# Start addresses of matmul operands in a transformer layer: three fillings in the pools

## The chip, the cores and the metric

The kernel runs on 1 core of a Trainium2 chip. The metric is the device time of one execution in microseconds (us). The kernel before takes 2929.12 us (median of 3 runs, 2928.11 to 2932.33).

## What is computed

One layer of a hybrid backbone over 1024 latent tokens of width 1024 with 256 context tokens, in float32. Cut to what matters here:

```python
p = h @ w_in                                    # h: modulated RMSNorm of x
att = neighbourhood_attention(q, k, v, k_ctx, v_ctx, rpb)
merged = (g0 * (att @ w_att_o) + g1 * (fourier @ w_fourier) + g2 * pooled)
x = x + gate1 * (merged @ w_out)
h2 = modulate(x, norm2_g, sh2, sc2)
affinity = softmax(h2 @ w_router)
gates, idx = lax.top_k(swapaxes(affinity, 1, 2), cap)   # 16 experts, 128 tokens each
xg = h2[idx]
a, u = xg @ w_gate[e], xg @ w_up[e]             # 1024 -> 2816
y = (silu(a) * u) @ w_down[e] * gates           # 2816 -> 1024
x = x + gate2 * scatter_add(y);  out = rmsnorm(x)
```

## The kernel before, in words

Every large product is made three times (lines 67 to 69, `mm3`): a float32 operand is split into a high part in the reduced type float32r and a remainder, and high x high, high x low, low x high are added up in PSUM. In a product one operand is stationary (128x128, loaded into the array) and one is moving (up to 512 columns are streamed past it).

A block of weights of 1 MB comes by DMA from the sync engine's queue into a raw buffer `wraw`; ScalarE casts it (line 62) and VectorE subtracts (line 63) into one of four buffers `whl` (high and low). The stages, in order of time:
- Projections, Fourier mixing, pooling, gates: the normed tokens `hT` (and `hcT` for the context) lie in SBUF in both parts. Most products have `hT` moving and `whl` stationary; for the values `whl` is moving and `hT` stationary.
- Attention, by head pairs.
- Merge (function `merge`): the attention's output is read back into tiles `at0` to `at7`, two pools of them (`attT0`, `attT1`, by halves of the tokens), as moving operand against `w_att_o` in `whl`. In the first chunk the first tile is read from a raw buffer of the ring instead. The sums, gated, go to `mg`; blocks of 128 tokens of it are split into `mhl`, the stationary operand of the product with `w_out` in `whl`. Then come norm, router and ranking; the ranking of groups of token blocks on VectorE runs beside the products of the next blocks.
- Experts (function `moe`): 16 experts one after the other. An expert's 128 rows are gathered (`xg`), transposed, modulated and split into `xT` (`turned`, 16 activations on ScalarE per expert but the first). The inner width 2816 goes in chunks of 512, the last of 256. Gate and up have `xT` stationary and `whl` moving; their gated product `a` is transposed on TensorE and split into `aT`, which is stationary for the down product with `whl` moving, into `y`. The result is scaled and added to the stream in memory by a scatter (line 1216, GpSimd), one per expert but the last. The loads run through a ring of 12 raw buffers, the splits 4 halves ahead. The order of TensorE, ScalarE and VectorE in this stage is written out by hand: the instructions stand in the order in which the loop calls for them.

Tiles lie in pools, each a run of bytes in every partition of SBUF. A tile's address follows from the pool's start and the tiles before it in the pool; pools on the right side grow from the top down. The names in the profile are the tiles' names without buffer numbers.

Of the kernel before, what the change touches and what calls it, by code (L numbers as in the profile page):

```python
# [9 lines left out]
F32 = mybir.dt.float32  # L10
# [24 lines left out]
def f(ap):  # L35
    return ap.bitcast(F32)


class Kernel:
# [13 lines left out]
    def pool(self, name, bufs=1, space=None, side=None):  # L53
        kw = {"reuse_waits": "tile"} if space != DRAM else {}
        if space is not None:
            kw["space"] = space
        if side is not None:
            kw["side"] = side
        return self.tc.tile_pool(name=name, bufs=bufs, **kw)

    def split(self, hi, lo, src, eng=None):
        self.nc.scalar.copy(hi, src)  # L62
        (eng or self.nc.vector).tensor_sub(lo, src, f(hi))  # L63
# [34 lines left out]
    def rstd(self, ss, pool, tag):  # L98

        nc = self.nc  # L100
        n = ss.shape[1]
        v = pool.tile([128, n], F32, name=tag + "v")
        s = pool.tile([128, n], F32, name=tag + "s")
        r = pool.tile([128, n], F32, name=tag + "r")
        nc.vector.tensor_scalar(v, ss, 1.0 / D, EPS, op0=ALU.mult, op1=ALU.add)
        nc.scalar.sqrt(s, v)
        nc.vector.reciprocal(r, s)
        nc.vector.tensor_mul(s, r, r)
        nc.vector.tensor_mul(s, s, v)
        nc.vector.tensor_scalar(s, s, -0.5, 1.5, op0=ALU.mult, op1=ALU.add)  # L110
        nc.vector.tensor_mul(r, r, s)
        return r
# [639 lines left out]
    def merge(self):  # L752
# [3 lines left out]
        self.tv = gates.tile([128, CB, NE, 4], F32R, name="tv")  # L756
        self.iota1 = gates.tile([128, 128], F32, name="iota1")
        with ExitStack() as st:
            rt = self.route_tiles(st.enter_context(self.pool("route")))
            mp = st.enter_context(self.pool("merged", side="right"))  # L760
            mg = [mp.tile([128, KT, 512], F32, name=f"mg{h}") for h in range(2)]
            xv = io["x"].rearrange("(r cb c) d -> cb r c d", r=R, cb=CB)
# [2 lines left out]
            def load(cb):  # L765
                mhl = hp.tile([128, 2, KT, 128], F32R, name="mhl")
                q = 128 * (cb % 4)
                self.split(mhl[:, 0], mhl[:, 1], mg[cb // 4][:, :, q:q + 128])
                tiles[cb] = mhl

            with ExitStack() as sa:
                ms = sa.enter_context(self.pool("msb", 2, side="right"))
                ap1 = sa.enter_context(self.pool("attT1", 1, side="right"))
                sa0 = sa.enter_context(ExitStack())
                ap0 = sa0.enter_context(self.pool("attT0", 1, side="right"))
                ps = sa.enter_context(self.pool("psa", 8, space=PSUM))
                for ch in range(2):
                    W = self.wchunk(io["w_att_o"], 512 * ch)
                    if ch == 0:
                        at0 = self.wraw.tile([128, 2048], F32R, name="wraw").rearrange("p (s t) -> p s t", s=2)  # L780
                        nc.sync.dma_start(f(at0), self.attd[0:128])
                        at = [[ap.tile([128, 2, 512], F32R, name=f"at{k}") for k in range(KT)]
                              for ap in (ap0, ap1)]
                        for k in [*range(1, KT), 0]:
                            for half in range(2):
                                nc.sync.dma_start(f(at[half][k]), self.attd[128 * k:128 * k + 128, :,
                                                                            512 * half:512 * half + 512])
                    units = [(b, half) for half in range(2) for b in range(4)]
                    acc = [ps.tile([128, 512], F32, name="mm") for _ in units]
                    order = [(k, u) for k in range(KT) for u in range(8)]  # L790
                    if ch:
                        order.sort(key=lambda ku: ku[1])
                    for k, u in order:
                        b, half = units[u]
                        p = acc[u]
                        i = 4 * ch + b
                        ws, ts = slice(128 * b, 128 * b + 128), slice(512 * half, 512 * half + 512)
                        a = at0[:, :, ts] if ch == k == 0 else at[half][k]
                        self.mm3(p, W(0, k)[:, ws], W(1, k)[:, ws], a[:, 0], a[:, 1], k == 0, k == KT - 1)
                        if k < KT - 1:  # L800
                            continue
                        sl = slice(128 * i, 128 * i + 128)
                        sg = ms.tile([128, 512], F32, name="sg")
                        pt = ms.tile([128, 512], F32, name="pt")
                        nc.sync.dma_start(sg, self.g1s[sl, ts])
                        nc.sync.dma_start(pt, self.part2[sl, ts])
                        nc.vector.tensor_mul(sg, p, sg)
                        nc.vector.tensor_add(mg[half][:, i], sg, pt)
                        if ch == 1 and u == 3:
                            sa0.close()  # L810
                            hp = st.enter_context(self.pool("mhl", 2))
                            w_out.append(self.wchunk(io["w_out"], 0))
                            load(0)
                            load(1)
            sp = st.enter_context(self.pool("x1", 2))
# [247 lines left out]
    def moe(self, upto):  # L1063
        nc, io = self.nc, self.io
        NR = RING
        with ExitStack() as st:
# [5 lines left out]
            sp = st.enter_context(self.pool("moe", 2))  # L1072
# [42 lines left out]
            def turned(ex, b, eng=None):  # L1115

                if b == 0:
                    ex.xT = sp.tile([128, 2, KT, 128], F32R, name="xT")
                scale, shift = self.mod2[:, 24:32], self.mod2[:, 0:8]
                tp = pst.tile([128, 512], F32, name="tp")  # L1120
                h32 = sp.tile([128, 512], F32, name="a")
                for k in range(4):
                    kk, cs = 4 * b + k, slice(128 * k, 128 * k + 128)
                    nc.tensor.transpose(tp[:, cs], ex.xg[:, 128 * kk:128 * kk + 128], self.ident)
                for k in range(4):
                    kk, cs = 4 * b + k, slice(128 * k, 128 * k + 128)
                    A, B = scale[:, kk:kk + 1], shift[:, kk:kk + 1]
                    nc.scalar.activation(ex.xT[:, 0, kk], tp[:, cs], AF.Identity, bias=B, scale=A)  # L1128
                    if eng is not None:
                        eng.tensor_scalar(h32[:, cs], tp[:, cs], A, B, op0=ALU.mult, op1=ALU.add)  # L1130
                    else:
                        nc.scalar.activation(h32[:, cs], tp[:, cs], AF.Identity, bias=B, scale=A)  # L1132
                nc.vector.tensor_sub(ex.xT[:, 1, 4 * b:4 * b + 4], h32.rearrange("p (k t) -> p k t", t=128),  # L1133
                                     f(ex.xT[:, 0, 4 * b:4 * b + 4]))
# [85 lines left out]
            def expert(e):  # L1220
                ex = Expert()
                ex.h, ex.aT = {}, {}
                ex.hot = choose_hot(e)
                return ex
# [8 lines left out]
            with self.pool("first", 1, side="right") as fp:  # L1233

                ex = expert(0)
# [6 lines left out]
            for b in range(2):  # L1242
                turned(ex, b, nc.vector)
# [7 lines left out]
            for j, (w, e, c, s) in enumerate(halves):  # L1251
                n = chunks[c][1]
                if (w, c, s) == ("w_gate", 0, 0) and e:
                    ex = nxt
# [23 lines left out]
                if (w, s) == ("w_gate", 0) and e + 1 < NE:  # L1278
                    if c == 2:
                        nxt = expert(e + 1)  # L1280
                        put(before, j + 3, lambda nx=nxt: choose_rows(nx))
                    if c == 4:
                        put(before, j + 1, lambda nx=nxt: turned(nx, 0))
                        put(before, j + 3, lambda nx=nxt: turned(nx, 1))
# [140 lines left out]
```

## Time and profile before

| | us |
|---|---|
| median of 3 runs | 2929.12 |
| lowest, highest | 2928.11, 2932.33 |
| profiled execution | 2928.25 |
| its span | 2926.5 |
| TensorE busy | 2811.0 |
| VectorE busy | 2040.7 |
| ScalarE busy | 1686.5 |
| GpSimd busy | 280.2 |

The span is the time from the first to the last instruction of the profiled execution. The stage of the experts takes the larger half of it, from 1334 us on. Matmuls are pipelined: a row of the timeline has the start of an instruction and how long it was in the engine, and the next one starts before it ends. So the engine's pace is read from the distance between starts. PE is TensorE, DVE VectorE, ACT ScalarE, POOL GpSimd, SPq the sync engine's DMA queue.

### The profile page before, as it was taken

The page shows a single profiled execution, that of the slowest core. Times are in us where ns is not written, and L with a number is a line of the kernel's source. Part 1 is how long each engine was busy: PE and PEld are TensorE (multiplying, and loading weights), DVE is VectorE, ACT ScalarE, POOL GpSimd, SP SyncE. Part 2 cuts the span into 40 slices and gives each one's busy share as a digit, 9 for nine tenths or more (in the row PEclk, how much of TensorE's full clock was granted, in tenths as well). Part 3 has the DMA queues.
Part 4 walks back from the last instruction along what each step waited for, and adds up shares of the span by engine and source line. Part 5 has one row for each costly group of instructions (what it writes and reads, how often), then busy time and mean ns, then how long its engine had stood idle before and what let it go on. Part 6 is the DMA issues. An engine that isn't in the chain of part 4 may idle for free.

```text
span 2926.5 us, 36071 instructions
## 1 busy us (share of the span) xinstructions
PE 2811.0 (96%) x13607; PEld 2304.4 (79%) x13607; DVE 2040.7 (70%) x2412; ACT 1686.5 (58%) x2005; POOL 280.2 (10%) x436
## 2 busy tenths in 40 slices
PE   7999999999999789987999999999999999999996
PEld 3888888887788777766888888888888888888885
DVE  4423232245578773478888988888888888988887
ACT  5412122212078771245777777777777777777775
POOL 1110000001144320000000000000000000000000
PEclk9999999999999899998999999999999999999998
DMA  8433231225877748558999999999999999999994
GB/s 250 175 124 144 79 123 66 104 80 167 272 190 193 184 140 284 156 166 309 338 362 369 375 367 360 370 376 365 358 367 382 365 361 360 385 364 360 362 383 175
DMA packets 346351, 783.54 MB, mean 268 GB/s; under 512 B 17288, under 2 KB 61008, under 8 KB 346048
## 3 DMA queue, kind: packets, MB, share of 16 engines
q1 hardware_dynamic: 326272, 713.48, 69.3%
q0 software_dynamic: 19664, 67.60, 6.9%
q8 instruction: 107, 1.75, 0.2%
q14 instruction: 68, 0.56, 0.1%
q10 hardware_dynamic: 240, 0.16, 0.0%
HBM read 710.37 MB, written 70.80 MB: 267 GB/s over the span
## 4 chain that ended last, share of the span: by engine, by line
PE 46%; ACT 4%; DVE 2%; issue 1%; DMA 1%; DVEq 0%
PE y L69 5%; PE y L68 5%; PE y L67 5%; PE w_gate L69 5%; PE w_gate L68 5%; PE w_gate L67 5%; PE w_up L67 5%; PE w_up L69 5%; PE w_up L68 5%; ACT whl L62 2%; PE tp L1202 1%; ACT a L1132 1%; ACT xT L1128 1%; DMA wraw<-in_w_up 1%; PE tp L1101 0%
## 5 line engine op out<-in xcount | busy, mean ns | idle before, releaser
L63 DVE TENSOR_TENSOR whl<-wraw,whl 128x2048 fp32r<-128x2048 f32 (+1 forms) x656 | 1295.1, 1997 | 240.4 <-ACT whl L62 236.3
L62 ACT CAST whl<-wraw 128x2048 fp32r<-128x2048 f32 (+1 forms) x660 | 1092.1, 1671 | 445.0 <-PE y L69 132.5
L68 PE MATMUL mm<-hT,whl 128*128 128x512 f32 x768 | 300.9, 392 | 1.6 <-DVE hT L273 1.6
L67 PE MATMUL mm<-hT,whl 128*128 128x512 f32 x768 | 300.2, 392 | 1.5 <-ACT hT L267 1.5
L69 PE MATMUL mm<-hT,whl 128*128 128x512 f32 x768 | 300.8, 392 | 0.0
L69 PE MATMUL w_gate<-whl,xT 128*128 128x512 f32 (+1 forms) x768 | 290.8, 379 | 2.8 <-DVE xT L1133 2.8
L67 PE MATMUL w_gate<-whl,xT 128*128 128x512 f32 (+1 forms) x768 | 292.1, 380 | 0.0
L67 PE MATMUL w_up<-whl,xT 128*128 128x512 f32 (+1 forms) x768 | 291.5, 380 | 0.0
L68 PE MATMUL w_gate<-whl,xT 128*128 128x512 f32 (+1 forms) x768 | 289.7, 377 | 0.0
L69 PE MATMUL w_up<-whl,xT 128*128 128x512 f32 (+1 forms) x768 | 289.1, 376 | 0.0
L68 PE MATMUL w_up<-whl,xT 128*128 128x512 f32 (+1 forms) x768 | 288.4, 375 | 0.0
L67 PE MATMUL y<-whl,aT 128*128 128x512 f32 x704 | 284.8, 405 | 0.0
L69 PE MATMUL y<-whl,aT 128*128 128x512 f32 x704 | 278.7, 396 | 0.0
L68 PE MATMUL y<-whl,aT 128*128 128x512 f32 x704 | 278.1, 395 | 0.0
L67 PEld LDWEIGHTS mm<-hT,whl 128*128 128x128 f32 x768 | 144.9, 189 | 37.8 <-ACT sg L529 5.2
L69 PEld LDWEIGHTS w_gate<-whl,xT 128*128 128x128 f32 x768 | 145.2, 189 | 32.2 <-DVE xT L1133 3.5
L68 PEld LDWEIGHTS mm<-hT,whl 128*128 128x128 f32 x768 | 145.3, 189 | 31.7 <-DVE hT L273 2.1
L69 PEld LDWEIGHTS mm<-hT,whl 128*128 128x128 f32 x768 | 145.2, 189 | 30.1
L68 PEld LDWEIGHTS w_gate<-whl,xT 128*128 128x128 f32 x768 | 145.0, 189 | 29.6
L69 PEld LDWEIGHTS w_up<-whl,xT 128*128 128x128 f32 x768 | 144.5, 188 | 29.1
L67 PEld LDWEIGHTS w_gate<-whl,xT 128*128 128x128 f32 x768 | 144.8, 189 | 28.4
L68 PEld LDWEIGHTS w_up<-whl,xT 128*128 128x128 f32 x768 | 144.3, 188 | 28.3
(354 smaller groups left out, 4333.1 us busy)
## 6 DMA issues: line engine op xcount, KB each, us to landing
wraw<-in_w_gate SPq DMA_DIRECT2D x160, 1024.0 KB, 11.1
wraw<-in_w_up SPq DMA_DIRECT2D x160, 1024.0 KB, 9.0
wraw<-in_w_down SPq DMA_DIRECT2D x160, 1024.0 KB, 11.8
wraw<-in_w_in SPq DMA_DIRECT2D x28, 1024.0 KB, 5.5
wraw<-in_ada_w SPq DMA_DIRECT2D x24, 1024.0 KB, 6.3
wraw<-in_w_gate SPq DMA_DIRECT2D x32, 512.0 KB, 11.4
wraw<-in_w_up SPq DMA_DIRECT2D x32, 512.0 KB, 8.5
wraw<-in_w_down SPq DMA_DIRECT2D x32, 512.0 KB, 4.9
```

The lines of the kernel that those rows point to most:

```text
L62: self.nc.scalar.copy(hi, src)
L63: (eng or self.nc.vector).tensor_sub(lo, src, f(hi))
L67: mm(out, lh, rh, start=start, stop=False, **kw)
L68: mm(out, lh, rl, start=False, stop=False, **kw)
L69: mm(out, ll, rh, start=False, stop=stop, **kw)
L1128: nc.scalar.activation(ex.xT[:, 0, kk], tp[:, cs], AF.Identity, bias=B, scale=A)
L1132: nc.scalar.activation(h32[:, cs], tp[:, cs], AF.Identity, bias=B, scale=A)
L1202: nc.tensor.transpose(tp[:, 128 * k:128 * k + 128], ex.ready[:, 128 * k:128 * k + 128], self.ident)
```

## The change

A method `fill` reserves a tile that nothing uses. It is called three times: 352 bytes at the end of the route tiles (ahead of all that is allocated after them in the merge, `mhl` among it), 416 bytes in the pool `msb` on the right side (below which the pools of `at` lie), and 352 bytes in the experts' pool, ahead of `xT`, once, with the first expert.

```diff
+    def fill(self, pool, size):
+        pool.tile([128, size // 4], F32, name="fill", bufs=1)
...
-            rt = self.route_tiles(st.enter_context(self.pool("route")))
+            rp = st.enter_context(self.pool("route"))
+            rt = self.route_tiles(rp)
+            self.fill(rp, 352)
...
                 ap1 = sa.enter_context(self.pool("attT1", 1, side="right"))
+                self.fill(ms, 416)
...
                 if b == 0:
+                    if ex.hot[0] == 0:
+                        self.fill(sp, 352)
                     ex.xT = sp.tile([128, 2, KT, 128], F32R, name="xT")
```

No instruction is added, removed or moved: on every engine and queue the built program has the same instructions in the same order with waits for the same semaphores. What differs is start addresses. The table has the byte at which an operand starts within a line of 512 bytes, as the built program has it; offsets within the tiles are whole lines in all of these.

| product (128 columns stationary) | products | moving, stationary | before | after |
|---|---|---|---|---|
| projections, 512 columns | 2304 | `hT`, `whl` | 64, 64 | 64, 64 |
| values, 512 columns | 480 | `whl`, `hT` or `hcT` | 64, 64 | 64, 64 |
| keys of the context, 256 columns | 192 | `hcT`, `whl` | 64, 64 | 64, 64 |
| pooling, 512 columns | 48 | `ph`, `wp` | 64, 320 | 64, 320 |
| attention output, first tile from the ring | 24 | `wraw`, `whl` | 480, 64 | 480, 64 |
| attention output | 360 | `at`, `whl` | 480, 64 | 64, 64 |
| merge with `w_out` | 384 | `whl`, `mhl` | 64, 224 | 64, 64 |
| experts' gate and up, 512 columns | 3840 | `whl`, `xT` | 64, 224 | 64, 64 |
| experts' gate and up, 256 columns | 768 | `whl`, `xT` | 64, 224 | 64, 64 |
| experts' down, 512 columns | 2112 | `whl`, `aT` | 64, 224 | 64, 64 |

Other tiles behind a filling move with it: `x1`, `xt`, `h2`, `g1b` of the merge and `a`, `yo` of the experts from 224 to 64, `x1T` (stationary in 64 router products of 16 columns) from 0 to 352.

## Rows read from the trace of the kernel before

**Rows 1.** Busy time: stretch, length, PE, PEld, DVE, ACT, POOL (instructions), clock, DMA share, GB/s.
```profile
1800.00:2300.00 500.00, 498.94 (x2366) 408.30 (x2365) 437.71 (x295) 380.01 (x340) 21.83 (x10) 1.00 1.01 367
```

**Rows 2.** Waits from 1400 to 2800 us: us in total, times, longest.
```profile
ACT whl L62 <- PE y L69: 120.3, 130, 2.1
...
SPq L1155 <- DVE whl L63: 934.2, 424, 5.3
```

**Rows 3.** Timeline of POOL: first and last scatter, 13 others between; start, us.
```profile
1460.82 3.41 POOL L1216 DMA_INDIRECT xacc<-yo,tok  x1 [76.96 <-DVE yo L1212]
...
2820.45 3.39 POOL L1216 DMA_INDIRECT xacc<-yo,tok  x1 [76.92 <-DVE yo L1212]
```

**Rows 4.** Timeline of PE, 340 to 380 us: first and last of 178.
```profile
339.83 0.39 PE L69 MATMUL mm<-hT,whl 128*128 128x512 f32 x1
...
379.95 0.39 PE L69 MATMUL mm<-hT,whl 128*128 128x512 f32 x1
```

**Rows 5.** Timeline of PE, 180 to 220 us: first and last of 178.
```profile
179.81 0.39 PE L68 MATMUL mm<-whl,hT 128*128 128x512 f32 x1
...
219.93 0.39 PE L68 MATMUL mm<-whl,hcT 128*128 128x512 f32 x1
```

**Rows 6.** Timeline of PE, 1110 to 1150 us: first and last of 173.
```profile
1109.66 0.40 PE L69 MATMUL mm<-at,whl 128*128 128x512 f32 x1
...
1149.96 0.39 PE L67 MATMUL mm<-at,whl 128*128 128x512 f32 x1
```

**Rows 7.** Timeline of PE, 1190 to 1208 us: first and last of 78.
```profile
1189.84 0.40 PE L68 MATMUL mm<-whl,mhl 128*128 128x512 f32 x1
...
1207.80 0.39 PE L67 MATMUL mm<-whl,mhl 128*128 128x512 f32 x1
```

**Rows 8.** Timeline of PE, 2865 to 2875 us, last expert: first and last of 44 products.
```profile
2864.70 0.39 PE L68 MATMUL w_gate<-whl,xT 128*128 128x512 f32 x1
...
2874.73 0.39 PE L69 MATMUL y<-whl,aT 128*128 128x512 f32 x1
```

**Rows 9.** Busy time in the stretches of rows 4 and 6 to 8; columns of rows 1.
```profile
340.00:380.00 40.00, 40.00 (x178) 33.10 (x178) 9.70 (x12) 8.09 (x11) 5.52 (x8) 1.00 0.41 146
...
1190.00:1208.00 18.00, 18.00 (x78) 14.48 (x78) 6.39 (x9) 1.70 (x2) 2.63 (x4) 1.00 0.47 171
1110.00:1120.00 10.00, 10.00 (x45) 8.03 (x44) 0.00 (x0) 0.00 (x0) 0.00 (x0) 1.00 1.05 387
2865.00:2875.00 10.00, 10.00 (x45) 7.99 (x44) 8.03 (x6) 5.37 (x5) 0.00 (x0) 1.00 0.00 0
```

**Rows 10.** Timelines of ACT and PE: the end of one expert.
```profile
2087.91 1.91 ACT L62 CAST whl<-wraw 128x2048 fp32r<-128x2048 f32 x1 [0.89 <-PE w_gate L69]
...
2099.55 0.40 PE L69 MATMUL y<-whl,aT 128*128 128x512 f32 x1
2100.13 0.63 PE L1202 MATMUL tp<-ident,a 128*128 128x128 f32 x4 [0.18 <-DVE a L1196]
```

**Rows 11.** Timeline of PE: 256 columns, 46 starts in the experts, 52 in the keys.
```profile
2103.76 0.28 PE L67 MATMUL w_gate<-whl,xT 128*128 128x256 f32 x1
...
2109.15 0.39 PE L67 MATMUL y<-whl,aT 128*128 128x512 f32 x1
...
162.84 0.28 PE L67 MATMUL mm<-hcT,whl 128*128 128x256 f32 x1
...
168.96 0.28 PE L67 MATMUL mm<-hcT,whl 128*128 128x256 f32 x1
```

**Rows 12.** Waits of DVE from 1240 to 1335 us.
```profile
DVE x L836 <- PE mm L69: 8.7, 6, 4.2
```

**Rows 13.** Busy time in 4 us inside an expert; columns of rows 1.
```profile
2030.00:2034.00 4.00, 4.00 (x19) 3.20 (x18) 3.90 (x3) 3.11 (x2) 0.00 (x0) 1.00 1.05 407
```

**Rows 14.** Timeline of PE: start of the products with `at`, 5 others between.
```profile
1101.41 0.79 PE L67 MATMUL mm<-at,whl 128*128 128x512 f32 x1 [2.97 <-DMA at<-attd]
...
1104.13 0.53 PE L67 MATMUL mm<-at,whl 128*128 128x512 f32 x1
```

## The prediction

> **What bounds the kernel now.** I read four views, in this order. The table of stretches says which engine is full: in the experts' stage TensorE (PE) is busy 498.94 of 500 us, VectorE (DVE) 437.71, ScalarE (ACT) 380.01, and the DMA engines carry 367 GB/s at a share of 1.01 [rows 1]. The waits say who is held by whom: ACT's casts of weights wait for PE to free a buffer (120.3 us behind `y` alone), and the load queue waits for DVE to free a slot of the ring (934.2 of 1400 us) [rows 2]. So loads and splits run ahead of PE, and PE's pace sets the time. The scatters, one per expert, give that pace: 14 periods between the first and the last shown, (2820.45 - 1460.82) / 14 = 97.1 us [rows 3]. The fourth view, PE's timeline, is the one that matters here. The change moves no instruction, only start addresses, so the question is whether a product's time depends on where its operands start. A row's duration does not tell, since products overlap; the distance from one start to the next does. I take it from the first and last start of an undisturbed stretch and the number of intervals between.
>
> **What a start address is worth.** All of these are products of 128x512, and the starts within a 512-byte line are those of the table in the section on the change.
> - Moving `hT` at 64, stationary `whl` at 64: 177 intervals, (379.95 - 339.83) / 177 = 226.7 ns [rows 4].
> - Moving `whl` at 64, stationary `hT` or `hcT` at 64, the roles as in the experts: (219.93 - 179.81) / 177 = 226.7 ns [rows 5].
> - Moving `at` at 480, stationary `whl` at 64: 172 intervals, (1149.96 - 1109.66) / 172 = 234.3 ns [rows 6].
> - Moving `whl` at 64, stationary `mhl` at 224: 77 intervals, (1207.80 - 1189.84) / 77 = 233.2 ns [rows 7].
> - Moving `whl` at 64, stationary `xT` or `aT` at 224: 43 intervals, (2874.73 - 2864.70) / 43 = 233.3 ns [rows 8].
>
> Equal starts give 226.7 ns in both roles, unequal ones 233 to 234. Other load does not explain it. The `at` stretch has 10 us in which DVE, ACT and GpSimd do nothing; the expert stretch has no DMA at all; and the `mhl` stretch (DVE 6.39 of 18 us, DMA 0.47) is loaded much like the `hT` stretch at 226.7 (DVE 9.70 of 40, DMA 0.41); the granted clock is 1.00 in all four [rows 9]. I therefore take 6.6 ns for an `xT`, `aT` or `mhl` product and 7.6 for an `at` product.
>
> A rule of the Trainium skill speaks against this. TensorE: Matmul & The Clock Gate, Part 2, on the steps of a matmul, says of the two read ports that "Loading the next tile's weights doesn't steal SBUF read bandwidth from the running matmul"; how the two addresses stand to each other would then not matter and the sum would be zero instead of what follows. Rows 4 to 8 do not agree with it as far as they go.
>
> **The sum.** All four moved kinds end at 64, the case of rows 4 and 5.
> - *Experts.* The page's counts less the 256-column forms leave 3840 + 2112 = 5952 products of 512 columns, 372 per expert (240 for gate and up, 132 for down), 2.46 us per expert if PE alone sets the time. It does not everywhere. Once per expert ACT turns the next expert's rows between casts: it begins a cast at 2087.91 that PE's last gate product of that half released, and what follows ends in the transpose on PE at 2100.13, which comes 0.58 us after the product at 2099.55, not 0.23: a stall of 0.35 us [rows 10]. In that stretch PE needs (2099.55 - 2087.91) / 0.2333 = 50 products; ACT's work there is not shortened, so PE only waits longer, by 50 x 6.6 ns = 0.33 us. I count 322 products, 2.13 us, for 14 experts: 29.8. The last expert turns nobody's rows: 2.46. The first begins with waits for its first splits; as an allowance I drop 58 products (a sixth) besides the 50: 264 x 6.6 ns = 1.7. Together 34.0 us.
> - *256-column products* (768). With `xT` at 224: 45 intervals, (2109.15 - 2103.76) / 45 = 119.8 ns. With equal starts (`hcT`, `whl` at 64): 51 intervals, (168.96 - 162.84) / 51 = 120.0 ns [rows 11]. I take nothing. The far end on one side is half of 226.7, 113.3 ns: 768 x 6.5 ns = 5.0 us gained; on the other 0.2 ns each, 0.2 us lost.
> - *Attention output, `at`.* 2 chunks x 8 x 8 units x 3 are 384 products, less 24 that use the ring's buffer as operand (it stays at 480), less some that follow a wait [rows 14]: about 350. 350 x 7.6 ns = 2.7 us, and what follows (the last sums, the split of `mhl`) starts that much earlier.
> - *Merge, `mhl`.* 384 x 6.5 ns = 2.5 us. From 1240 us on DVE's ranking runs beside them; it waits for these products 8.7 us, in 6 waits [rows 12], so most of the gain reaches it. I take 2.0, between 1.5 (half is lost after 1240) and 2.5.
> - *Other tiles that move.* `x1T` goes the other way, 0 to 352: 64 router products, bounded by 7.6 ns each, 0.5 us either way, taken as nothing. The 16 activations of the ACT stretch write moved tiles; no row compares them, and if they changed by 3% as the products do, 16 x 0.35 us x 3% = 0.17 us per expert, 2.6 us in all, either way; taken as nothing. The fillings themselves are memory only.
>
> Sum: 34.0 + 2.7 + 2.0 = 38.7 us off the profiled execution's 2928.25 (span 2926.5), 2889.6. The median shown is 0.9 above that execution, so I forecast **2890.5**.
>
> What hides the rest must still hold. DVE: 437.71 of 500 us becomes 437.71 of 489, 90%. DMA: 367 GB/s x 97.1 / 94.97 = 375 GB/s; a 4 us stretch of the same loads moves 407 GB/s [rows 13], and the ring is ahead by the waits of rows 2.
>
> **The rivals.**
> - *Half is given back.* The experts' loads cannot go much faster. One expert needs 97.1 us x 367 GB/s = 35.6 MB; with a limit of 372 GB/s its period is 95.8 instead of 95.0 us, so 15 x 1.3 = 20 us and 4.7 from the merge remain: 2904. For it: a DMA share of 1.01. Against it: 407 GB/s in rows 13. A longer ACT stretch would look the same.
> - *The change does nothing.* The 6.6 ns come from something that these stages have and the projections lack, other than the start bytes; then 2929. For it: no row has the expert's own shapes at equal starts. Against it: rows 5 have the same roles, and rows 9 take load away. By the rule of the skill quoted above this is what should happen.
> - *Slower: a longer wait in the ACT stretch, and slow products behind it.* Place: the transpose behind the ACT stretch, once in each of 15 experts. After a wait of 3 us for `at`, the next products start (1104.13 - 1101.41) / 6 = 453 ns apart, and 7 of them cost 7 x 0.22 = 1.5 us more than usual [rows 14]. If the stall grew from 0.35 to 3 us, each expert would lose 2.65 + 1.5 us, 62 in all, against 38.7 gained: 2952. It decides from 2.6 us per expert, wait and slow products together. For it: ACT is without a pause there. Against it: I find 0.33 us added, not 2.65, and behind today's 0.35 us the stage as a whole keeps a granted clock of 1.00 [rows 1].
>
> **How the numbers follow.** The forecast has 0.82, half given back 0.11, nothing 0.04, slower 0.02; 0.01 is left. About 0.2% of this kernel, 6 us, is what a measurement tells from no change. Faster by more than that takes in the first two and the rest: 0.94; within it 0.04; slower 0.02. The range begins at 2878: 5952 x 6.6 ns = 39.3, with 2.7, 2.5 and the 5.0 of the 256-column products make 49.5, and 2928.25 - 49.5 is 2878.8. It ends at 2906, where the case of half given back lies, with 2 us for the activations.
>
> **What would show it.** Right: in the stages of rows 6, 7 and 8 starts 226.7 ns apart; the scatters 95.0 us apart; the transpose behind the ACT stretch waiting about 0.7 us; 256-column products still at 120 ns; DMA near 375 GB/s. Wrong: starts that stay at 233 ns (then the start bytes were not the cause), or starts at 227 ns with a period above 95.5 us; then the waits before PE, by DMA, by DVE's splits or by ACT, show which cover is gone.

## The result, and the profile after

The changed kernel takes **2895.14 us** (median of 4 runs, 2893.53 to 2896.83) against 2928.61 us for the kernel before in the same comparison: 0.9884 of its time, 95% interval [0.9869, 0.99]. The forecast was 2890.5, in a range of 2878 to 2906. The profiled execution took 2896.28 us (span 2894.5). Lines of the program stand 5 to 10 higher than before; L72 to L74 are now the three products of `mm3`.

PE's timeline has most of the answer. The stretches are, in order: `at` (152 starts), `mhl` (83), the first expert's first product, the end of the ScalarE stretch in one expert, 256 columns (48), and a piece of the last expert behind transposes (`tp`), with 72 products from 2826.76 on.

```profile
1109.89 0.39 PE L72 MATMUL mm<-at,whl 128*128 128x512 f32 x1
...
1144.11 0.39 PE L73 MATMUL mm<-at,whl 128*128 128x512 f32 x1
...
1188.75 0.39 PE L73 MATMUL mm<-whl,mhl 128*128 128x512 f32 x1
...
1207.33 0.39 PE L74 MATMUL mm<-whl,mhl 128*128 128x512 f32 x1
...
1329.74 0.80 PE L72 MATMUL w_gate<-whl,xT 128*128 128x512 f32 x1
...
1700.09 0.39 PE L74 MATMUL y<-whl,aT 128*128 128x512 f32 x1
1700.87 0.63 PE L1212 MATMUL tp<-ident,a 128*128 128x128 f32 x4 [0.39 <-DVE a L1206]
...
2085.73 0.28 PE L72 MATMUL w_gate<-whl,xT 128*128 128x256 f32 x1
...
2091.37 0.28 PE L74 MATMUL w_up<-whl,xT 128*128 128x256 f32 x1
...
2826.40 0.60 PE L1212 MATMUL tp<-ident,a 128*128 128x128 f32 x4
2826.76 0.48 PE L72 MATMUL y<-whl,aT 128*128 128x512 f32 x1
2827.07 0.40 PE L73 MATMUL y<-whl,aT 128*128 128x512 f32 x1
...
2829.61 0.39 PE L72 MATMUL w_gate<-whl,xT 128*128 128x512 f32 x1
...
2842.99 0.39 PE L74 MATMUL y<-whl,aT 128*128 128x512 f32 x1
```

- `at`: (1144.11 - 1109.89) / 151 = 226.6 ns; it was 234.3 [rows 6]. `mhl`: (1207.33 - 1188.75) / 82 = 226.6 ns; it was 233.2 [rows 7]. `xT` and `aT`, once settled: (2842.99 - 2829.61) / 59 = 226.8 ns; they were at 233.3 [rows 8].
- The eleven distances right behind the transposes are longer, although all operands start at 64: (2829.61 - 2827.07) / 11 = 230.9 ns. This was not foreseen.
- 256 columns: (2091.37 - 2085.73) / 47 = 120.0 ns, as before [rows 11].
- Behind the ScalarE stretch the transpose stands 0.78 us behind the last product, a stall of 0.55 us where there were 0.35 [rows 10].

The scatters give the experts' period. Timeline of POOL, first and last of 15:

```profile
1454.61 3.41 POOL L1226 DMA_INDIRECT xacc<-yo,tok  x1 [75.50 <-DVE yo L1222]
...
2790.19 3.39 POOL L1226 DMA_INDIRECT xacc<-yo,tok  x1 [75.49 <-DVE yo L1222]
```

(2790.19 - 1454.61) / 14 = 95.4 us, down from 97.1 [rows 3]; 95.0 was forecast. Of the 32.0 us by which the span fell, 4.4 lie ahead of the experts (their first product begins at 1329.74, not at 1334) and 27.6 within their stage; the tail behind the experts is as long as it was.

Busy time in the stretch of [rows 1]:

```profile
1800.00:2300.00 500.00, 498.00 (x2415) 415.96 (x2414) 447.29 (x298) 387.92 (x335) 21.82 (x10) 1.00 1.02 375
```

and the waits from 1400 to 2800 us (us in total, times, longest):

```profile
ACT whl L67 <- PE y L74: 115.1, 131, 2.2
...
PE tp L1212 <- DVE a L1206: 6.0, 15, 0.4
...
SPq L1165 <- DVE whl L68: 958.6, 434, 5.1
```

PE is still full, DMA moves 375 GB/s, casts and loads still wait for buffers as in [rows 2]. The one wait of PE that the view lists is the stall behind the ScalarE stretch, 15 times.

### The profile page after: what moved, and what is told of

Same layout as the page of the kernel before. It is cut to its first block, busy times and chain, and to the rows that moved or that the text cites. A ratio compares the mean times of both kernels' runs of the same rounds, so it can differ in the third digit from the quotient of the medians.

```text
span 2894.5 us, 36071 instructions
## 1 busy us (share of the span) xinstructions
PE 2774.9 (96%) x13607; PEld 2303.0 (80%) x13607; DVE 2038.0 (70%) x2412; ACT 1686.1 (58%) x2005; POOL 279.6 (10%) x436
## 4 chain that ended last, share of the span: by engine, by line
PE 45%; DMA 3%; DVE 3%; ACT 3%; issue 1%; DVEq 0%
PE y L72 5%; PE y L74 5%; PE y L73 5%; PE w_gate L74 5%; PE w_gate L72 5%; PE w_gate L73 5%; PE w_up L72 5%; PE w_up L74 4%; PE w_up L73 4%; DMA wraw<-in_w_up 3%; PE tp L1212 1%; ACT whl L67 1%; DVE whl L68 1%; ACT xT L1138 1%; DMA wraw<-in_w_down 0%
## 5 line engine op out<-in xcount | busy, mean ns | idle before, releaser
L72 PE MATMUL mm<-hT,whl 128*128 128x512 f32 x768 | 300.3, 392 | 1.5 <-ACT hT L272 1.5
L74 PE MATMUL mm<-hT,whl 128*128 128x512 f32 x768 | 301.2, 392 | 0.0
L74 PE MATMUL w_gate<-whl,xT 128*128 128x512 f32 (+1 forms) x768 | 286.9, 374 | 2.8 <-DVE xT L1143 2.8
L72 PE MATMUL w_gate<-whl,xT 128*128 128x512 f32 (+1 forms) x768 | 289.5, 377 | 0.0
L72 PE MATMUL w_up<-whl,xT 128*128 128x512 f32 (+1 forms) x768 | 288.7, 376 | 0.0
L73 PE MATMUL w_gate<-whl,xT 128*128 128x512 f32 (+1 forms) x768 | 286.3, 373 | 0.0
L74 PE MATMUL w_up<-whl,xT 128*128 128x512 f32 (+1 forms) x768 | 286.0, 372 | 0.0
L73 PE MATMUL w_up<-whl,xT 128*128 128x512 f32 (+1 forms) x768 | 285.6, 372 | 0.0
L72 PE MATMUL y<-whl,aT 128*128 128x512 f32 x704 | 282.4, 401 | 0.0
L74 PE MATMUL y<-whl,aT 128*128 128x512 f32 x704 | 275.5, 391 | 0.0
L73 PE MATMUL y<-whl,aT 128*128 128x512 f32 x704 | 275.2, 391 | 0.0
L72 PEld LDWEIGHTS mm<-hT,whl 128*128 128x128 f32 x768 | 145.0, 189 | 37.3 <-ACT sg L534 5.2
L74 PEld LDWEIGHTS mm<-hT,whl 128*128 128x128 f32 x768 | 145.4, 189 | 30.0
L74 PEld LDWEIGHTS w_gate<-whl,xT 128*128 128x128 f32 x768 | 145.1, 189 | 29.0 <-DVE xT L1143 3.5
L74 PEld LDWEIGHTS w_up<-whl,xT 128*128 128x128 f32 x768 | 144.8, 188 | 25.6
L72 PEld LDWEIGHTS w_gate<-whl,xT 128*128 128x128 f32 x768 | 145.3, 189 | 24.7
```

What stands on the lines that cost most here:

```text
L72: mm(out, lh, rh, start=start, stop=False, **kw)
L73: mm(out, lh, rl, start=False, stop=False, **kw)
L74: mm(out, ll, rh, start=False, stop=stop, **kw)
```

## The experiments

For the price of a product three theories had to be told apart: *equal starts in a 512-byte line* matter (mine), *the distance between the two starts* does, counted in some smaller unit, or *the start of one operand alone*. For the part of the gain that is missing: *breaks* (products behind a transpose are slow until they have settled) or *reading engines* (ScalarE and VectorE read `tp` just then). And for the stall: whether it can be had back.

### One part of the change alone

`experts_only` keeps the filling ahead of `xT` and drops the two others; `merge_only` does the reverse.

```diff
 experts_only:
-            self.fill(rp, 352)
-                self.fill(ms, 416)
 merge_only:
-                    if ex.hot[0] == 0:
-                        self.fill(sp, 352)
```

> Of the three fillings only the one in the experts' pool is kept: xT and aT start at 64 as in the changed kernel, at stays at 480 and mhl at 224. If the three fillings act apart from each other, each on its own products: the experts' stage takes 95.4 us per expert as in the changed kernel, the merge is as before, and the gain is the 27.6 us by which the experts' stage became shorter, some 2901 us. The rival, that a good part of the gain comes from something the fillings do together (the distance between pools, the buffers of the ring): well under 27 us.

> Of the three fillings only the two of the merge are kept: at and mhl start at 64, xT and aT at 224 as before. If the fillings act apart: the first expert starts 4.4 us earlier, as in the changed kernel, each expert takes 97.1 us, and the gain is 4.4 us, some 2924.5 us. The rival, that this part is not seen because the ranking on VectorE takes it back: no difference from before.

Measured in one comparison (before: 2928.87 us): the experts alone 2902.58 us, 0.9907 [0.9892, 0.9922], with a period of 95.4 us; the merge alone 2925.02 us, 0.9984 [0.9975, 0.9993], with a period of 97.1 us and the first expert's product at 1331.4. The two parts give 26.3 and 3.9 us, 30.2 together; the whole change gave 33.5, 28.9 and 31.6 in its three comparisons. They add up, as expected, and most of what is missing from the 38.7 us forecast lies in the experts.

### Other distances

Two kernels put the moved operands at other bytes, one moves `whl` as well, by 32 bytes. Only the fillings' sizes differ from the change; `fill2` stands ahead of the first `aT`.

```diff
 off_a:  rp 480, ms 384, sp 416, + self.fill(sp, 192, "fill2")
 off_b:  rp 384, ms 160, sp 608, + self.fill(sp, 32, "fill2")
 whl_32:
                 self.whl = s2.enter_context(self.pool("whl2", 4))
+                self.fill(self.whl, 32)
```

> Other fillings put each operand at another byte, with whl at 64: xT at 128 (64 apart), aT at 320 (256 apart), mhl at 192 (128 apart), at at 96 (32 apart). Theory of the line: only the same byte of a 512-byte line helps, so all four keep starts of 233 to 234 ns, some 2928 us. Theory of the 64 bytes: a distance that is a multiple of 64 is enough, so xT, aT and mhl products start 226.7 ns apart away from the transposes, only at stays at 234, and the time is that of the changed kernel plus 2.7 us, some 2898 us. Theory of the single operand (each has to start at a multiple of 64 by itself) expects the same as that of the 64 bytes here.

> With whl at 64: xT at 320 (256 apart), aT at 352 (288 apart, that is 32 beyond a multiple of 64), mhl at 96 (32 apart), at at 320 (256 apart). Theory of the line: all four at 233 to 234 ns. Theories of the 64 bytes and of the single operand: xT and at at 226.7 ns, aT and mhl at 233; the time some 15 us above the changed kernel (2112 products of aT x 6.6 ns, 384 of mhl x 6.5), about 2910 us.

> A filling of 32 bytes ahead of whl in the merge and the experts: whl, mhl, xT and aT now all start at 96, so they are at the same byte, but none at a multiple of 64; at stays at 64, 32 away from whl. Theories of the line and of the 64 bytes (it is the distance that counts): the products of mhl, xT and aT keep 226.7 ns away from the transposes, at goes to 234, some 2898 us. Theory of the single operand: all of them at 233, some 2929 us.

Measured by the timelines of PE, as above: (last start - first start) / intervals, away from transposes or once settled behind them.

| kernel | operands (start bytes in a line of 512) | distance | ns per product |
|---|---|---|---|
| change | `at`, `mhl`, `xT`, `aT` 64; `whl` 64 | 0 | 226.6 to 226.8 |
| whl_32 | `mhl`, `xT`, `aT` 96; `whl` 96 | 0 | 226.7, 226.8 |
| whl_32 | `at` 64; `whl` 96 | 32 | 233.3 |
| off_a | `at` 96; `whl` 64 | 32 | 233.3 |
| off_b | `mhl` 96; `whl` 64 | 32 | 233.3 |
| off_a | `xT` 128; `whl` 64 | 64 | 233.4 |
| off_a | `mhl` 192; `whl` 64 | 128 | 233.3 |
| before | `mhl`, `xT`, `aT` 224; `whl` 64 | 160 | 233.2, 233.3 |
| off_b | `aT` 352; `whl` 64 | 288 | 232.7 |
| off_a | `aT` 320; `whl` 64 | 256 | 226.7 |
| off_b | `xT`, `at` 320; `whl` 64 | 256 | 226.6, 226.7 |
| before | `at` 480; `whl` 64 | 416 | 234.3 |

The rows of it that decide, first from `off_a` (`xT` at distance 64, 48 products; then `aT` at 256, the last 16 of 24 products behind transposes):

```profile
2856.92 0.40 PE L72 MATMUL w_gate<-whl,xT 128*128 128x512 f32 x1
...
2867.89 0.39 PE L74 MATMUL w_up<-whl,xT 128*128 128x512 f32 x1
...
2884.69 0.39 PE L74 MATMUL y<-whl,aT 128*128 128x512 f32 x1
...
2888.09 0.39 PE L74 MATMUL y<-whl,aT 128*128 128x512 f32 x1
```

from `off_b` (`xT` at 256, 48 products, and `aT` at 288, 12):

```profile
2837.58 0.39 PE L72 MATMUL w_gate<-whl,xT 128*128 128x512 f32 x1
...
2848.23 0.40 PE L74 MATMUL w_up<-whl,xT 128*128 128x512 f32 x1
2848.47 0.39 PE L72 MATMUL y<-whl,aT 128*128 128x512 f32 x1
...
2851.03 0.39 PE L74 MATMUL y<-whl,aT 128*128 128x512 f32 x1
```

and from `whl_32` (`xT` at 0, both operands at 96; 48 products):

```profile
2836.22 0.39 PE L72 MATMUL w_gate<-whl,xT 128*128 128x512 f32 x1
...
2846.88 0.39 PE L74 MATMUL w_up<-whl,xT 128*128 128x512 f32 x1
```

The start of one operand alone falls: with `whl` 32 bytes on, `at` at 64 is slow and `xT` at 96 fast. That the starts have to be equal within 512 bytes falls too: 256 apart is as good as 0. So does a unit of 64 bytes: 64 and 128 apart are as slow as the rest. What all twelve cases have in common is that a distance which is a multiple of 256 bytes gives 226.7 ns and every other one tried (32, 64, 128, 160, 288, 416) 232.7 to 234.3. The times of these single runs go in the same order: 2923.98 us where only `aT` is right, 2904.56 where `xT` and `at` are, 2902.97 where all but `at` are (before beside them: 2930.88). The experts' periods tell it more cleanly, since the start of the first expert varies by several us from kernel to kernel (1330.1 us in `off_b`, 1335.9 in `whl_32`): (2816.68 - 1463.82) / 14 = 96.6 us in `off_a`, (2797.89 - 1455.49) / 14 = 95.9 in `off_b` and (2796.81 - 1460.84) / 14 = 95.4 in `whl_32`, against 97.1 before and 95.4 with the change.

The trace of before already had a case that speaks against equal starts. The 48 products of the pooling, three in a row each time, have `ph` at 64 and `wp` at 320, 256 apart, and they start at the pace of the `hT` products around them:

```profile
634.53 0.39 PE L69 MATMUL mm<-hT,whl 128*128 128x512 f32 x1
634.75 0.39 PE L67 MATMUL mm<-ph,wp 128*128 128x512 f32 x1
634.98 0.39 PE L68 MATMUL mm<-ph,wp 128*128 128x512 f32 x1
635.21 0.39 PE L69 MATMUL mm<-ph,wp 128*128 128x512 f32 x1
```

`off_a` shows one thing more. Where its `aT` products follow its slow `xT` products directly, with no transpose between, the first eight distances between them are 230.0 ns on average (62 places from 1400 us on) and the next three 226.7: here too products settle only after some eight.

### More transposes

A transpose whose result nobody reads is put ahead of the up products of three chunks per expert.

```diff
+                if (w, s) == ("w_up", 0) and c in (0, 1, 3):
+                    tp = pst.tile([128, 512], F32, name="tp")
+                    nc.tensor.transpose(tp[:, :128], self.iota1, self.ident)
                 products(j, ex)
```

> The changed kernel with one more transpose on TensorE (of a constant, into a buffer of tp that nothing reads) ahead of the first half of up in chunks 0, 1 and 3 of each expert, 48 in all, at places where no other transpose is near. In the changed kernel the first dozen products behind a run of transposes start 227 to 234 ns apart instead of 226.7. Theory of the interruption: whatever breaks the row of equal products puts weight loads and moving reads out of step, so behind the added transposes too some ten products start 227 to 234 ns apart, and each costs 0.11 us for itself, 0.09 for the product behind it and 0.03 to 0.05 for the slow ones: 48 x 0.24 = 11 us, about 2907 us. Rival: the products are slow there since ScalarE and VectorE read the transposes' result and write aT at that time; then the products behind the added transposes, which nobody reads, are back at 226.7 ns at once, about 9.5 us.

Measured: 2899.61 us in a single run (before: 2930.88), and a period of (2793.30 - 1453.40) / 14 = 95.7 us instead of 95.4. One such transpose in the timeline of PE:

```profile
2787.68 0.27 PE L1269 MATMUL tp<-ident,iota 128*128 128x128 f32 x1
2787.71 0.48 PE L72 MATMUL w_up<-whl,xT 128*128 128x512 f32 x1
2788.03 0.39 PE L73 MATMUL w_up<-whl,xT 128*128 128x512 f32 x1
...
2789.64 0.39 PE L74 MATMUL w_up<-whl,xT 128*128 128x512 f32 x1
...
2793.04 0.39 PE L74 MATMUL w_up<-whl,xT 128*128 128x512 f32 x1
```

The seven distances behind the second product are (2789.64 - 2788.03) / 7 = 230.0 ns, the 15 after them (2793.04 - 2789.64) / 15 = 226.7. Over all 45 added transposes from 1400 us on the distances at places 1 to 5 behind the first product are 231.7, 233.0, 228.3, 229.0 and 228.7 ns, and from place 7 on 226.6 to 227.2. No engine reads the added transposes, so a break by itself slows the products behind it; that the reading engines alone do it falls. Whether they add to it is not shown: over places 1 to 9 an added break costs 19 ns above 226.7 ns per product, one of the program's own, mostly of four transposes that are read, 33 ns in the changed kernel (its means are given below). Both sizes expected for the time were too large: by the periods an added break costs 0.3 / 3 = 0.1 us, 48 of them 5 us.

### The stall behind the ScalarE stretch

First the obvious try: four of the eight activations per half go to VectorE, for the second half (`turn_dve`) or for both (`turn_both`, the same edit in the line of `turned(nx, 0)` too), beside the changed kernel once more.

```diff
-    put(before, j + 3, lambda nx=nxt: turned(nx, 1))
+    put(before, j + 3, lambda nx=nxt: turned(nx, 1, nc.vector))
```

> The changed kernel once more, on the chip of the next two runs, as their base. Expected: 2895 us, 0.988 to 0.989 of the kernel before.

> The change, and four of the eight activations that turn the second half of the next expert's rows go from ScalarE to VectorE. Theory (the wait behind the ScalarE stretch is what kept part of the expected gain: PE's transpose there waits about 0.55 us, 15 times): the wait is gone, the transpose stands as far behind the last product as everywhere else, the period falls from 95.4 to 94.9 us and the time by 15 x 0.55 = 8 us to about 2887. Rival (that stretch has several chains of about the same length: VectorE's product of the gated halves stands behind the same instructions, now on VectorE): the transpose waits as long as before or longer, and the time stays at 2895 or rises by up to 8 us.

> As the run before, and the first half's four activations go to VectorE as well. Theory (ScalarE's stretch sets the wait): no more than the run before, about 2887, since the wait can go only once. Rival (VectorE is the next bound in the stretch; it gets eight more instructions beside its subtractions): the splits of weights come late and PE waits for them, 2890 to 2900 us.

Measured in one comparison (before: 2927.73 us): the change 2898.85 us, 0.9901 [0.9884, 0.9918]; `turn_dve` 2957.73, 1.0095 [1.0078, 1.0112]; `turn_both` 3004.04, 1.0258 [1.0241, 1.0276]. The theories were wrong; the rivals were right in that a wait remains, but made it far too small. In `turn_both` the transpose waits up to 4.9 us for VectorE's gated product, 68.7 us in 14 times, and the period is 102.4 us. Timelines of ScalarE and VectorE in `turn_dve` show how its wait comes about:

```profile
2005.47 0.46 ACT L1138 ACTIVATE xT<-tp,mod 128x128 fp32r<-128x128 f32 x1 [2.03 <-DVE a L1140]
2006.41 0.46 ACT L1138 ACTIVATE xT<-tp,mod 128x128 fp32r<-128x128 f32 x1 [0.48 <-DVE a L1140]
...
2005.96 0.41 DVE L1140 TENSOR_SCALAR a<-tp,mod 128x128 f32<-128x128 f32 x1 [0.53 <-ACT xT L1138]
```

Both read the same tile `tp`, and in this program they take turns: a pair costs 2006.41 - 2005.47 = 0.94 us, where ScalarE alone, in the changed kernel, starts its two 0.35 us apart:

```profile
1696.46 0.51 ACT L1138 ACTIVATE xT<-tp,mod 128x128 fp32r<-128x128 f32 x1
1696.81 0.51 ACT L1142 ACTIVATE a<-tp,mod 128x128 f32<-128x128 f32 x1
```

The Trainium skill has the reason for building it so (PSUM — Partial Sum Buffer, "PSUM bank collisions raise a hardware error"): two engines must not access one bank, in the same quarter of the partitions, at once, two reads included; the rows agree in that no two of these instructions overlap. ScalarE, which has the casts of the next weights behind them, also waits 2.03 us until VectorE, still at its subtractions, has come to the first of them. The bill comes on PE:

```profile
2006.55 0.39 PE L74 MATMUL y<-whl,aT 128*128 128x512 f32 x1
2009.72 0.95 PE L1212 MATMUL tp<-ident,a 128*128 128x128 f32 x4 [2.78 <-ACT whl L67]
2010.33 0.77 PE L72 MATMUL y<-whl,aT 128*128 128x512 f32 x1
...
2013.39 0.39 PE L73 MATMUL y<-whl,aT 128*128 128x512 f32 x1
```

After a wait of 2.78 us the next seven products start (2013.39 - 2010.33) / 7 = 437 ns apart. Busy time in that stretch:

```profile
2009.70:2013.20 3.50, 3.48 (x11) 2.91 (x12) 2.75 (x3) 0.59 (x1) 0.00 (x0) 0.52 0.76 231
```

The granted clock is 0.52, that is near the lower level of 1.2 GHz, after PE had stood idle. The period is (2847.08 - 1454.12) / 14 = 99.5 us, 4.1 more than the change's.

Then the other way. The transpose waits for the gated product `a` (L1206) on VectorE, and that stands behind a subtraction for `xT`, which waits for ScalarE's activations. VectorE's timeline in the changed kernel, ahead of the transpose at 1700.87:

```profile
1699.44 0.69 DVE L1143 TENSOR_TENSOR xT<-a,xT 128x512 fp32r<-128x512 f32 x1 [0.80 <-ACT a L1142]
1700.05 0.68 DVE L1206 TENSOR_TENSOR a<-a,w_up 128x512 f32<-128x512 f32 x1
```

`late_low` puts the subtraction behind the gated product, and nothing else is moved:

```diff
+                    if c == 4 and e + 1 < NE:
+                        nxt.low()
...
-                        put(before, j + 3, lambda nx=nxt: turned(nx, 1))
+                        put(before, j + 3, lambda nx=nxt: turned(nx, 1, late=True))
```

(`low` is `turned`'s last statement, which `late` leaves out there; `gated(ex, n)` stands right ahead of the first two lines.)

> The changed kernel once more, on the chip of the next run, as its base. Expected: 0.988 to 0.990 of the kernel before, experts 95.4 us apart, the transpose behind the ScalarE stretch waiting 0.55 us in each.

> The change, and one subtraction of VectorE (the low part of the second half of the next expert's xT) stands behind the product of the gated halves instead of ahead of it, once per expert; nothing else moves. The gated product then no longer stands behind ScalarE's eight activations. Theory (the wait behind the ScalarE stretch is held by this order on VectorE alone, and costs its 0.55 us plus nothing else): the transpose stands 0.23 us behind the last product like everywhere else, the period falls from 95.4 to 94.9 us, the time by 15 x 0.5 = 7 to 8 us against the run of the same chip. Rival (ScalarE's stretch also holds the casts for the next products, so PE waits a little later for the same reason): the transpose's wait goes, another wait of the same size stands at the next product with a new whl or aT, and the time stays within 2 us.

Measured in one comparison (before: 2931.72 us): the change 2900.10 us, 0.9886 [0.9869, 0.9902]; `late_low` **2889.66 us** (2886.68 to 2893.80), 0.9857 [0.984, 0.9873]. PE's timeline behind the ScalarE stretch:

```profile
1700.18 0.39 PE L74 MATMUL y<-whl,aT 128*128 128x512 f32 x1
1700.41 0.60 PE L1215 MATMUL tp<-ident,a 128*128 128x128 f32 x4
```

POOL's first and last of 15 scatters:

```profile
1455.84 3.41 POOL L1229 DMA_INDIRECT xacc<-yo,tok  x1 [74.94 <-DVE yo L1225]
...
2783.32 3.39 POOL L1229 DMA_INDIRECT xacc<-yo,tok  x1 [74.92 <-DVE yo L1225]
```

The transpose follows after 0.23 us, the view of PE's waits from 1400 to 2800 us lists none any more, and the period is (2783.32 - 1455.84) / 14 = 94.8 us. Against the 95.4 us of the change, 15 x 0.6 = 9 us, of the 10.4 between the medians. This is the fastest of all kernels here.

## Why the prediction was right, and where it was off

**The start address.** Right in size and place: `at`, `mhl`, `xT` and `aT` all came to 226.6 to 226.8 ns, and the loads, ring and splits followed. The reason was too narrow: the starts need not be equal, a distance of 256 bytes is as good, and the pooling's products in the trace of before could have said so.

**The term that was mis-sized** is the one of the experts, 34.0 us where 27.6 came. It gave 6.6 ns to every one of 372 products per expert and took off only the stall. Each expert has nine breaks by transposes, and in this the program is unlike the projections from which the price came. Worked out from the starts of ten experts before and after (from 1527.6 us on), the 353 distances per expert from one 512-column product to the next, without the first behind each break, went from 233.4 to 227.7 ns, that is 2.01 us; with the rest of PE's row but for its waits it is 2.05, where 2.46 were counted. By place behind a break, mean of 90: 230.9, 232.8, 233.8, 227.6, 230.6, 232.2, 227.2, 229.6, 228.3 and then 226.3 to 227.4, but for 230.9 at place 13, where one distance in nine is that of the third product behind the 256 columns (264 to 269 ns; 277 before); before, 231 to 237 at every place. 0.41 us for each of 15 experts are 6.2 of the 6.4 us that were missing. The experiment with added breaks shows that a break does this, if in smaller size. The trace of before held a hint: products of `whl` with `ahl` in the Fourier mixing, both at 64, stand 229.6 ns apart over the 70 distances that follow the first ones behind breaks, and 226.7 in the one stretch that goes on for longer. The prediction read unbroken stretches alone.

**The stall** was expected to grow by 0.33 us, from 0.35 to 0.68, and grew to 0.55. The mechanism was right, and `late_low` shows its worth: about 0.6 us per expert. By the means of ten experts it grew by 0.22 us; another 0.1 us went where the prediction saw nothing: the four transposes of the second chunk begin 0.28 us behind the last product instead of 0.23, and their starts spread over 0.38 us instead of 0.33. VectorE's gated product ends only 0.05 us ahead of them there (1552.52 and 1552.57 us; before 0.29, 1560.45 and 1560.74), so it may hold them; no run tests it. The 0.33 us came in sum, then, from two places: 2.05 - 0.33 = 1.72 us per expert, which is the fall of the period.

**The merge** was to give 4.7 us; the first expert begins 4.4 earlier, and the merge alone gives 3.9 by the medians. That is as near as it can be told: in three profiled executions of the changed kernel the first expert begins at 1329.7, 1330.8 and 1333.2, and in `experts_only`, whose merge is that of before, at 1332.4. The pace of the products, 226.6 ns in both stretches, is the firmer sign.

**256 columns** gain nothing, as taken: 120.0 ns.

**The covers held.** VectorE is at 447.29 of 500 us (90% was forecast), DMA at 375 GB/s, as forecast.

**The rivals.** *Half is given back* by a limit of DMA: it named 372 GB/s and 95.8 us; measured are 375 and 95.4, loads still wait for buffers, and `late_low`, with a period of 94.8, is faster still. What was given back, a fifth, went another way. *The change does nothing* falls with every stretch above; so does, for this case, what the prediction read out of the rule in TensorE: Matmul & The Clock Gate, Part 2, of the Trainium skill, that weight loads take no read bandwidth from the running product: that addresses don't matter. Whether it is the weight load that slows the product, no run shows. *Slower* didn't come, but `turn_dve` ran into just that place: its wait of 2.78 us and slow products behind it cost 4.1 us per expert, where the rival had priced 2.65 + 1.5.

**What stays open** is why. The runs show that the distance decides and that the pace takes some products to settle, not what in the chip makes it so. Not tried: further distances, such as 192 or 384 bytes; other lengths of break; and why 256 columns don't care.

## What to carry to other kernels

Look at where the stationary and the moving operand of long rows of products start: a distance that is a multiple of 256 bytes was worth 3% of each 128x512 product here, and some hundred bytes of filling buy it. Price such a gain from stretches that are broken as often as the ones it will be used in, since some ten products behind each break get only part of it. And when an engine at its limit stalls for a short time, look for what stands ahead of the awaited instruction on the other engine's queue before work is moved: reordering one subtraction gave 10 us, moving four instructions lost 59.

## What was not expected of the hardware

- It is the distance between the two starts that counts: 226.7 ns at 0 and 256 bytes (within a line of 512), 232.7 to 234.3 ns at 32, 64, 128, 160, 288 and 416.
- Products at a good distance need some six to ten products to reach 226.7 ns: behind transposes (230.9, 232.8, 233.8 ns at first), behind an added transpose that nobody reads (231.7, 233.0, 228.3), and behind products at a bad distance (230.0 on average over eight).
- ScalarE and VectorE taking turns on one PSUM tile need 0.94 us for two instructions that ScalarE alone starts 0.35 us apart.
